# One-hots taken off VectorE, and 104 more gathered rows ordered ahead of the dense stage, in a decoder layer kernel

## The chip, the cores and the metric

The kernel runs on one core of a Trainium2 chip. The metric is the device time of one execution, in microseconds. The engines have short names here: PE is TensorE (the matmuls, with PEld its weight loads), DVE is VectorE, ACT is ScalarE, POOL is GpSimd, and SP is SyncE, which issues most plain DMAs. Each engine works through its own queue in order, and waits at an instruction until what that instruction needs has been done by the others.

## The reference

One decoder layer on 1024 tokens of width 1024: two kinds of attention in parallel, and then a retrieval layer with 16384 experts, each of which is one row of `peer_u` and one row of `peer_v`. Cut to what matters here:

```python
h = h + concat(mla(...), diff_attn(...)) @ w_out          # attention, 8 tiles of 128 tokens
x = rms_norm(h, ffn_norm)
# per token and head (8 heads): 16 experts out of 128 x 128, by a product of two lists of keys
best, flat = top_k(s1[..., :, None] + s2[..., None, :], 16)
experts = e1 * 128 + e2                                   # (token, 8 heads, 16)
g   = softmax(best)
act = gelu(einsum('cd,chkd->chk', x, u[experts]))         # 128 dot products per token
h   = h + einsum('chk,chkd->cd', g * act, v[experts])     # 128 weighted rows per token
```

So each token has 128 chosen experts, each with two keys `e1` and `e2` below 128 and a gate `g`.

## The kernel before

The 1024 tokens are 8 tiles of 128. The expert layer is done in two ways.

**Sparse tiles 0, 1, 6 and 7** (`sparse`, lines 938 to 983) gather the chosen rows. For each of the 128 choices, POOL issues an indirect DMA that brings one row of 1024 numbers to each of the 128 tokens (`gather`, line 957, 512 KB), and DVE makes the dot product with the token (`dot`, line 963); then the same over `peer_v`, where DVE adds the weighted row to a sum (`add`, line 975). One tile is a list of 259 entries: `begin`, 128 dots, `turn`, 128 adds, `end`. There are six row buffers, and two more in the dense stage, so POOL can run only that many rows ahead of DVE.

**Dense tiles 2 to 5** (`dense`, lines 985 to 1099) multiply all 512 tokens with all the experts on PE, 128 experts (one `e1`) at a time: 24 matmuls for the activations (line 1021) and 24 for the weighted sum (line 1055), each of 512 columns, 6144 in all. Around each `e1` DVE splits the loaded rows into high and low parts (lines 1017, 1043 and 1048) and multiplies by the gates (line 1039).

The dense stage needs the gates as a full table over (expert, token). `scatter` (lines 901 to 936) builds it ahead of that stage. For eight tokens at a time DVE compares `e2` with 0 to 127 (line 908, the tile `late_gq`, 128x1024). `place` then handles four tokens: for each it makes a one-hot of `e1` that is scaled by the gate (a 128x128 tile, `late_o`), and one matmul (line 928) of the two one-hots gives the token's gates; ACT copies the four results out (line 211, `late_st`), and from time to time SP stores them to the DRAM table `GD`. Of the four scaled one-hots one is made on POOL and two on DVE (both line 926), and one on ACT by a Square and a Relu (lines 923 and 924). There are 4 tiles x 32 places = 128 places, and eight `late_o` buffers, which is two places' worth.

**What sets the order.** The lists of work are woven together by `interleave`, in stages: `attend` and `mix` of the tile groups, projections, places, and a share of the sparse list. `some(share)` takes `int(share * 259)` more entries of the sparse list, by the table `SHARES`, as far as the tiles are ready. The program that the engines get is then ordered by a scheduler, which may put a row that is ready ahead of work that was written before it. The dense stage can start in earnest only when the last place has been stored. `choose` of tiles 6 and 7, the rest of the key search for those tiles, runs beside the last places and into the start of the dense stage; its small products on POOL have line 832.

Of the kernel before, what the change touches and what calls it, by code (L numbers as in the profile page):

```python
# [15 lines left out]
OP = mybir.AluOpType  # L16
# [37 lines left out]
PIN = 1  # L54
ROWS = 6
ROWS2 = 2
SHARES = [0.4,0.3,0.3,0.3,0.3,0.3,0.1,0.1]


def shape_constants():  # L60
# [34 lines left out]
def interleave(*streams):  # L95

    todo = []
    for st in streams:
        if st:
            c = [getattr(f, "cost", 1.0) for f in st]  # L100
            todo.append([0, 0.0, sum(c), list(st), c])
    total = sum(len(x[3]) for x in todo)
    for _ in range(total):
        x = min((x for x in todo if x[0] < len(x[3])), key=lambda x: (x[1] + x[4][x[0]]) / x[2])
        x[3][x[0]]()
        x[1] += x[4][x[0]]
        x[0] += 1
# [3 lines left out]
def layer(ctx, tc, a):  # L111
    nc = tc.nc
    ve, sc, pe, gp, sy = nc.vector, nc.scalar, nc.tensor, nc.gpsimd, nc.sync
# [59 lines left out]
    seg_start, seg_dstart, iota16, iota128 = c128[:, :16], c128[:, 16:32], c128[:, 32:48], c128[:, 48:]  # L173
# [36 lines left out]
    def evac(out, in_):  # L210
        sc.activation(out, in_, AF.Copy)  # L211
# [689 lines left out]
    def scatter(t):  # L901
        v = {}

        def one_hots(i0):

            full = [128, 8, 128]
            v["sq"] = GC(full)
            ve.tensor_tensor(v["sq"], iota128[:, None, :].to_broadcast(full),  # L908
                             ET[t][:, 1, i0:i0 + 8, None].to_broadcast(full), op=OP.is_equal)

        def place(i0):
            eT = ET[t]
            if i0 % STG == 0:
                v["st"] = ST()
            if i0 % 8 == 0:
                one_hots(i0)
            st, sq = v["st"], v["sq"][:, i0 % 8:i0 % 8 + 4]
            pg = MM().rearrange("p (i n) -> p i n", n=128)
            o1s = [O1() for _ in range(4)]
            for i in range(4):  # L920
                col = lambda n: eT[:, n, i0 + i:i0 + i + 1]
                if i == 1:
                    sc.activation(o1s[i], iota128, AF.Square, bias=col(3))
                    sc.activation(o1s[i], o1s[i], AF.Relu, bias=col(2), scale=col(4))
                else:
                    (ve if i else gp).tensor_scalar(o1s[i], iota128, col(0), col(2), op0=OP.is_equal, op1=OP.mult)  # L926
            for i in range(4):
                pe.matmul(pg[:, i], sq[:, i], o1s[i], start=True, stop=True)  # L928
            s0 = i0 % STG
            evac(st[:, :, s0:s0 + 4], pg.rearrange("p i e -> p e i"))  # L930
            if s0 == STG - 4:
                tg = (DENSE.index(t) * 128 + i0) // STG
                q, tg = divmod(tg, TD // STG // 4)
                sy.dma_start(GD[:, q, :, tg].rearrange("c p e i -> p c (e i)"),
                             st.rearrange("p (c e) i -> p c (e i)", e=GE))

        return [lambda i0=i0: place(i0) for i0 in range(0, 128, 4)]

    more_rows, n_row = [], [0]
# [160 lines left out]
    def first(kind, st):  # L1100
        off = HP.get(kind, 0)
        if not off:
            return st

        def run(f):
            with tc.high_priority(off):
                f()
        return [lambda f=f: run(f) for f in st]
# [23 lines left out]
    def some(share):  # L1132
        lo, done[0] = done[0], min(259 * sum(t in IDXED for t in SPARSE), done[0] + int(share * 259))
        return lookups[lo:done[0]]
# [13 lines left out]
    interleave(attend(GROUPS[0]) + mix(GROUPS[0], ch), P[1])  # L1148
    interleave(attend(GROUPS[1]), P[2] if last > 1 else [], some(SHARES[0]))
    d2 = []  # L1150
    for g in range(1, last + 1):
# [14 lines left out]
        def delayed(st, f):  # L1166
            return [lambda: None] * int(f * len(st) / (1 - f)) + st if f >= 0 else st + [lambda: None] * int(-f * len(st) / (1 + f))
        interleave(first("m%d" % g, delayed(mix(GROUPS[g]) + (picks(g) if g < last else []), MD)),
                   first("a%d" % g, delayed(attend(GROUPS[g + 1]), AD)) if g < last else [],
                   first("p%d" % g, delayed(P[g + 2], PD)) if g + 2 < len(P) else [], first("b%d" % g, wait + tt + made), some(SHARES[g]))  # L1170
    fin = [f for t in SPARSE if t not in IDXED for f in choose(t)]
# [51 lines left out]
```

## Time and profile before

| | us |
|---|---|
| median of 3 runs | 3104.34 |
| lowest and highest | 3099.56 and 3111.25 |
| the profiled execution | 3106.77 |
| its span, first to last instruction | 3104.9 |

Busy shares over the whole span: PE 91%, PE weight loads 68%, DVE 81%, ACT 32%, POOL 57%. These are averages over stages with different limits. A windows table gives, for stretches of the span, the busy time of every engine with the number of its instructions in brackets, and then the granted TensorE clock (1.00 is 2.4 GHz), the share of time that the DMA engines were busy, and their GB/s. A group of instructions has a line of the kernel, an engine, an operation, `out<-in` names, shapes and a count; then busy time and the mean length of one in ns; and behind the bar the time that the engine stood idle just ahead of them, with what ended it.

### The profile page before, as it was taken

The numbers are of one execution on the slowest core, as the hardware profiler recorded it, in microseconds if no ns is written. First come the engines' busy times: TensorE is split into PE (matmuls) and PEld (weight loads), VectorE is DVE, ScalarE is ACT, GpSimd is POOL, SyncE is SP. The second block draws the span as 40 slices with busy tenths as digits, with TensorE's granted clock in tenths as the row PEclk, the third lists the DMA queues.
The fourth block names the chain that finished last, engine by engine and source line by source line (L and its number), as shares of the span: only waits on it lengthen the run. The fifth ranks groups of instructions, "written<-read, shape, count | busy, mean of one in ns | idle before, by whom it ended". The sixth has DMA issues, their size and how long they took to land.

```text
span 3104.9 us, 38301 instructions
## 1 busy us (share of the span) xinstructions
PE 2834.8 (91%) x12574; PEld 2125.7 (68%) x12574; DVE 2509.4 (81%) x5183; ACT 1002.0 (32%) x2030; POOL 1766.8 (57%) x1405
## 2 busy tenths in 40 slices
PE   7897889998897796889887999999999999999997
PEld 2555455565655673577676888788888877888885
DVE  1238775788999889976998997988888879888898
ACT  1413333322332342245573223222222222232221
POOL 2116673556557755741585764765555547666565
PEclk9698878998998897789998999999999999999998
DMA  7369897989989988954658998999999989999998
GB/s 214 108 236 312 300 328 254 347 304 315 324 282 319 316 303 269 333 182 149 214 170 288 350 361 311 342 374 346 338 351 342 351 278 386 350 351 342 339 345 312
DMA packets 371951, 934.35 MB, mean 301 GB/s; under 512 B 53365, under 2 KB 134393, under 8 KB 371753
## 3 DMA queue, kind: packets, MB, share of 16 engines
q0 software_dynamic: 147456, 536.94, 48.1%
q1 hardware_dynamic: 224296, 394.98, 37.0%
q8 instruction: 99, 1.62, 0.2%
q14 instruction: 100, 0.81, 0.1%
HBM read 871.80 MB, written 59.99 MB: 300 GB/s over the span
## 4 chain that ended last, share of the span: by engine, by line
PE 57%; DVE 16%; DMA 5%; issue 4%; POOL 3%; ACT 1%; DVEq 0%; POOLq 0%; ACTq 0%; SPq 0%
PE pa L1021 21%; PE acc L1055 16%; PE pa L1055 5%; PE mm L748 3%; DVE row L963 3%; PE sc L564 2%; PE mm L359 2%; DVE acc L975 2%; POOL row L957 2%; DVE late_o L926 2%; DMA row<-in_peer_u,idx 2%; DVE late_gq L908 1%; PE mm L594 1%; PE mm L928 1%; DMA skt<-in_sub_keys_t 1%
## 5 line engine op out<-in xcount | busy, mean ns | idle before, releaser
L957 POOL DMA_INDIRECT row<-in_peer_v,idx x512 | 680.3, 1329 | 479.5 <-DVE acc L975 312.5
L957 POOL DMA_INDIRECT row<-in_peer_u,idx x512 | 689.3, 1346 | 421.0 <-DVE row L963 224.7
L975 DVE SCALAR_TENSOR_TENSOR acc<-row,w,acc 128x1024 f32<-128x1024 f32 x512 | 668.6, 1306 | 10.4 <-DMA row<-in_peer_v,idx 5.9
L963 DVE SCALAR_TENSOR_TENSOR row<-row,xn 128x1024 f32<-128x1024 f32 x512 | 624.3, 1241 | 33.3 <-DMA row<-in_peer_u,idx 31.7
L1021 PE MATMUL pa<-xTh,us 128*128 128x512 f32 x2048 | 501.2, 393 | 17.0 <-DVE us L1017 15.1
L1021 PEld LDWEIGHTS pa<-xTh,us 128*128 128x128 f32 x2048 | 387.8, 190 | 100.0 <-DVE us L1017 16.2
L1055 PE MATMUL acc<-vh,al 128*128 128x512 f32 x768 | 301.7, 393 | 10.2 <-DVE al L1043 10.2
L1037 ACT ACTIVATE ga<-pa 128x512 f32<-128x512 f32 x128 | 76.6, 598 | 710.9 <-PE pa L1021 707.4
L1055 PE MATMUL acc<-vl,ah 128*128 128x512 f32 x768 | 300.6, 391 | 0.0
L1055 PE MATMUL acc<-vh,ah 128*128 128x512 f32 x768 | 270.1, 391 | 5.0 <-ACT ah L1042 5.0
L748 PE MATMUL mm<-xyT,slab 128*128 128x256 f32 (+1 forms) x1280 | 255.2, 353 | 5.5 <-DMA slab<-in_peer_w_query 4.4
L1021 PE MATMUL pa<-xTl,us 128*128 128x512 f32 x1024 | 254.6, 390 | 0.0
L359 PE MATMUL mm<-slab,nT 128*128 128x512 f32 x512 | 239.1, 613 | 1.0 <-ACT pc L211 0.9
L564 PE MATMUL sc<-kh,qh 96*128 96x512 f32 (+9 forms) x416 | 191.6, 574 | 49.1 <-ACT p L576 36.8
L748 PEld LDWEIGHTS mm<-xyT,slab 128*128 128x128 f32 x1280 | 212.4, 200 | 34.7 <-DMA slab<-in_peer_w_query 6.3
L926 POOL TENSOR_SCALAR late_o<-c,eT 128x128 f32<-128x128 f32 x128 | 148.1, 1160 | 137.2 <-PE mm L928 135.8
L1021 PEld LDWEIGHTS pa<-xTl,us 128*128 128x128 f32 x1024 | 193.5, 189 | 40.6
L1017 DVE TENSOR_TENSOR us<-raw,us 128x1024 fp32r<-128x1024 f32 x128 | 157.5, 1230 | 66.5 <-PE pa L1021 39.9
L1047 ACT ACTIVATE vh<-rv 128x1024 fp32r<-128x1024 f32 x128 | 132.8, 1053 | 191.1 <-PE pa L1055 143.5
L205 POOL TENSOR_TENSOR y<-v,neghalf 128x8 f32<-128x8 f32 (+6 forms) x68 | 92.8, 1365 | 173.1 <-DVE v L204 169.2
L1055 PEld LDWEIGHTS acc<-vh,al 128*128 128x128 f32 x768 | 145.2, 189 | 43.9 <-DVE al L1043 13.7
L928 PE MATMUL mm<-late_o,late_gq 128*128 128x128 f32 x1024 | 150.2, 291 | 23.4 <-POOL late_o L926 8.0
(249 smaller groups left out, 4651.1 us busy)
## 6 DMA issues: line engine op xcount, KB each, us to landing
raw<-in_peer_u_t SPq DMA_DIRECT2D x128, 512.0 KB, 6.7
rv<-in_peer_v SPq DMA_DIRECT2D x128, 512.0 KB, 6.8
slab<-in_peer_w_query SPq DMA_DIRECT2D x80, 512.0 KB, 7.5
slab<-in_w_in SPq DMA_DIRECT2D x64, 512.0 KB, 6.9
GD<-late_st SPq DMA_DIRECT2D x16, 2048.0 KB, 9.5
gc<-GD SPq DMA_DIRECT2D x16, 2048.0 KB, 14.7
slab<-in_w_out SPq DMA_DIRECT2D x40, 512.0 KB, 6.6
row<-in_peer_u,idx POOLq DMA_INDIRECT x512, 7.4
```

The lines of the kernel that those rows point to most:

```text
L359: pe.matmul(p, nT[t][:, k], w(k), start=(k == 0), stop=(k == 7))
L564: pe.matmul(at(lo, hi), qt, kt[:, lo:hi], start=True, stop=not ex)
L748: pe.matmul(p, w["q"](k)[:, j * 128:j * 128 + 128], st["xT"][:, k, :NG], start=(k == 0), stop=(k == 7))
L926: (ve if i else gp).tensor_scalar(o1s[i], iota128, col(0), col(2), op0=OP.is_equal, op1=OP.mult)
L928: pe.matmul(pg[:, i], sq[:, i], o1s[i], start=True, stop=True)
L957: gp.indirect_dma_start(out=r, out_offset=None, in_=a[name], in_offset=bass.IndirectOffsetOnAxis(ap=IDX[t][:, j:j + 1], axis=0))
L963: ve.scalar_tensor_tensor(r, r, 1.0, v["x"], op0=OP.mult, op1=OP.mult, accum_out=v["act"][:, j:j + 1])
L975: ve.scalar_tensor_tensor(v["y"], r, wj, v["y"], op0=OP.mult, op1=OP.add)
L1017: ve.tensor_tensor(ul, ur, uh.bitcast(F32), op=OP.subtract)
L1021: pe.matmul(pa, l[:, k], r[:, k], start=(i == 0 and k == 0), stop=(i == 2 and k == 7))
L1047: sc.activation(vh, vr, AF.Copy)
L1055: pe.matmul(out, l[:, ts], r[:, hf:hf + 512], start=(first and n == 0), stop=(last and n == 2))
```

## The change

Two things. `SHARES` gives other shares of the sparse list to the stages ahead of the dense one: 103 + 90 + 90 + 103 + 129 = 515 entries where it was 103 + 4 x 77 = 411. Entry 515 is the 126th add of tile 1, so 510 of the 512 rows of tiles 0 and 1 are written ahead, against 406 before. And in `place` the two scaled one-hots that DVE made go elsewhere: tokens 0 and 2 to POOL, tokens 1 and 3 to ACT.

```diff
-SHARES = [0.4,0.3,0.3,0.3,0.3,0.3,0.1,0.1]
+SHARES = [0.4,0.35,0.35,0.4,0.5]
@@ place
-                if i == 1:
+                if i % 2:
                     sc.activation(o1s[i], iota128, AF.Square, bias=col(3))
                     sc.activation(o1s[i], o1s[i], AF.Relu, bias=col(2), scale=col(4))
                 else:
-                    (ve if i else gp).tensor_scalar(o1s[i], iota128, col(0), col(2), op0=OP.is_equal, op1=OP.mult)
+                    gp.tensor_scalar(o1s[i], iota128, col(0), col(2), op0=OP.is_equal, op1=OP.mult)
```

In POOL's queue, around the 75th of the 128 places (line 832 is the key search, line 926 a one-hot, line 957 a gathered row of tile 1), before:

```order
L926 TENSOR_SCALAR late_o_12303<-c_94,eT 128x128
L926 TENSOR_SCALAR late_o_12323<-c_94,eT 128x128
L832 TENSOR_TENSOR oh<-oh,d_13665 128x512
L926 TENSOR_SCALAR late_o_12338<-c_94,eT 128x128
L926 TENSOR_SCALAR late_o_12370<-c_94,eT 128x128
L832 TENSOR_TENSOR oh<-oh,d_13665 128x512
```

The same place in POOL's queue of the changed kernel:

```order
L957 DMA row<-in_peer_v,idx_6579 128x1024
L926 TENSOR_SCALAR late_o_12583<-c_94,eT 128x128
L957 DMA row<-in_peer_v,idx_6579 128x1024
L926 TENSOR_SCALAR late_o_12585<-c_94,eT 128x128
L957 DMA row<-in_peer_v,idx_6579 128x1024
L832 TENSOR_TENSOR oh<-oh,i1f 128x512
L926 TENSOR_SCALAR late_o_12614<-c_94,eT 128x128
L957 DMA row<-in_peer_v,idx_6579 128x1024
L926 TENSOR_SCALAR late_o_12616<-c_94,eT 128x128
```

Two one-hots for each place stand where one stood, with rows of tile 1 between them. From the first row of tile 1's adds to the last one-hot, POOL's queue held 28 rows, 110 one-hots, 28 products of line 832 and 4 of line 205; now it holds 132 rows, 220 one-hots and the same 28 and 4.

DVE's queue at the last places, before:

```order
L908 TENSOR_TENSOR late_gq<-c_94,eT 128x1024
L926 TENSOR_SCALAR late_o_13381<-c_94,eT 128x128
L926 TENSOR_SCALAR late_o_13382<-c_94,eT 128x128
L908 TENSOR_TENSOR late_gq<-c_94,eT 128x1024
L926 TENSOR_SCALAR late_o_13398<-c_94,eT 128x128
L926 TENSOR_SCALAR late_o_13399<-c_94,eT 128x128
```

The same place now:

```order
L908 TENSOR_TENSOR late_gq<-c_94,eT 128x1024 x4
L762 MAX s_12383<-qc 128x8 x4
L764 MAX_INDEX i_12384<-s_12383,qc 128x8 x4
L766 MATCH_REPLACE qc<-s_12383,qc 128x128 x4
L908 TENSOR_TENSOR late_gq<-c_94,eT 128x1024
L768 MAX s_12383<-qc 128x8 x4
L770 MAX_INDEX i_12384<-s_12383,qc 128x8 x4
L908 TENSOR_TENSOR late_gq<-c_94,eT 128x1024 x9
```

DVE is left with the comparison for each eight tokens; no one-hot of line 926 is in its queue any more.

DVE's queue at the end of the program, before:

```order
L1069 TENSOR_TENSOR yacc<-yacc,pa 128x512 x2
L975 SCALAR_TENSOR_TENSOR acc_22411<-row_24443,w,acc_22411 128x1024
L975 SCALAR_TENSOR_TENSOR acc_22411<-row_24452,w,acc_22411 128x1024
L975 SCALAR_TENSOR_TENSOR acc_22411<-row,w,acc_22411 128x1024 x6
L975 SCALAR_TENSOR_TENSOR acc_22411<-row_24515,w,acc_22411 128x1024
L975 SCALAR_TENSOR_TENSOR acc_22411<-row_24522,w,acc_22411 128x1024
L1076 TENSOR_TENSOR rv<-rv,acc 128x1024
```

Now:

```order
L1039 TENSOR_TENSOR ga<-ga,gc 128x512
L1043 TENSOR_TENSOR al<-ga,ah 128x512
L1076 TENSOR_TENSOR rv<-rv,acc 128x1024 x2
L1069 TENSOR_TENSOR yacc<-yacc,pa 128x512 x2
L1076 TENSOR_TENSOR rv<-rv,acc 128x1024
```

The ten adds behind the last dense sum are gone from the end: the last row of tile 7 now stands some 18 of the 128 `e1` steps ahead of it.

## Rows read from the trace of the kernel before

**Rows 1.** Windows by stage: us, busy time of each engine (instructions), clock, DMA
```profile
1018.00:1258.00 240.00, 189.99 (x941) 142.24 (x940) 214.95 (x709) 80.16 (x192) 153.40 (x116) 0.85 0.88 297
1258.00:1641.00 383.00, 327.54 (x1992) 275.22 (x1991) 316.19 (x1011) 207.63 (x504) 212.31 (x170) 0.91 0.62 203
1641.00:1710.00 69.00, 49.91 (x196) 39.07 (x195) 60.15 (x166) 21.04 (x27) 34.92 (x22) 0.85 0.84 304
1710.00:3084.00 1374.00, 1360.75 (x5962) 1121.71 (x5960) 1204.45 (x1431) 384.89 (x493) 840.44 (x597) 0.99 0.93 344
```

**Rows 2.** Chain that ended last, in order of time: start, length, what (steady dense stage)
```profile
2049.43 5.44 PE pa L1021 x24
...
2103.38 4.08 PE acc L1055 x18
```

**Rows 3.** Groups of POOL from 1258 to 1641: busy, mean ns, idle before
```profile
L926 POOL TENSOR_SCALAR late_o<-c,eT 128x128 f32<-128x128 f32 x110 | 126.1, 1150 | 126.2 <-PE mm L928 125.2
L957 POOL DMA_INDIRECT row<-in_peer_v,idx x28 | 38.2, 1363 | 17.6 <-DVE acc L975 4.5 <-issue 3.6 <-DVE t L206 2.6
L832 POOL TENSOR_TENSOR oh<-oh,i1f 128x512 f32<-128x512 f32 x16 | 23.9, 1496 | 7.4 <-DVE oh L830 6.6 <-DVE t L206 0.6
L832 POOL TENSOR_TENSOR oh<-oh,d 128x512 f32<-128x512 f32 x12 | 20.7, 1725 | 11.8 <-DVE oh L830 11.8
L205 POOL TENSOR_TENSOR y<-v,neghalf 128x1 f32<-128x1 f32 (+1 forms) x4 | 3.8, 954 | 7.6 <-DVE v L204 7.6
```

**Rows 4.** Lines 926 and 957: count, shortest/median/longest ns, first and last start
```profile
L926 POOL TENSOR_SCALAR late_o<-c,eT x128: 780/871/2697, 1017.8 to 1639.8; 128x128 f32<-128x128 f32 x128
L957 POOL DMA_INDIRECT row<-in_peer_v,idx x512: 932/1144/4012, 590.6 to 3090.2; - x171
```

**Rows 5.** Windows of line 926 alone: us, DVE busy, POOL busy, clock, DMA
```profile
1018.00:1100.00 82.00, 5.39 (x16) 12.48 (x9) 0.85 0.88 302
...
1340.00:1486.00 146.00, 22.48 (x73) 37.64 (x38) 0.93 0.46 146
...
1591.00:1641.00 50.00, 19.83 (x62) 39.81 (x30) 0.97 0.56 174
```

**Rows 6.** Timeline of POOL in the last places: start, length, what
```profile
1624.50 0.87 POOL L926 TENSOR_SCALAR late_o<-c,eT 128x128 f32<-128x128 f32 x1 [0.73 <-PE mm L928]
1625.62 4.43 POOL L926 TENSOR_SCALAR late_o<-c,eT 128x128 f32<-128x128 f32 x3 [0.25 <-PE mm L928]
```

**Rows 7.** Timeline of DVE there
```profile
1624.88 0.60 DVE L926 TENSOR_SCALAR late_o<-c,eT 128x128 f32<-128x128 f32 x2 [1.03 <-PE mm L928]
1625.40 1.22 DVE L908 TENSOR_TENSOR late_gq<-c,eT 128x1024 f32<-128x1024 f32 x1
1626.54 1.11 DVE L926 TENSOR_SCALAR late_o<-c,eT 128x128 f32<-128x128 f32 x4
1627.56 1.22 DVE L908 TENSOR_TENSOR late_gq<-c,eT 128x1024 f32<-128x1024 f32 x1
```

**Rows 8.** Groups of DVE from 1258 to 1641
```profile
L926 DVE TENSOR_SCALAR late_o<-c,eT 128x128 f32<-128x128 f32 x220 | 77.5, 391 | 39.9 <-PE mm L928 39.7
L908 DVE TENSOR_TENSOR late_gq<-c,eT 128x1024 f32<-128x1024 f32 x54 | 65.6, 1215 | 0.0
L830 DVE TENSOR_TENSOR oh<-pf,c 128x512 f32<-128x512 f32 x28 | 19.1, 683 | 0.2
```

**Rows 9.** Groups of ACT from 1258 to 1641
```profile
L924 ACT ACTIVATE late_o<-late_o,eT 128x128 f32<-128x128 f32 x110 | 53.5, 487 | 0.5
L923 ACT ACTIVATE late_o<-c,eT 128x128 f32<-128x128 f32 x110 | 43.8, 398 | 17.2 <-PE mm L928 16.3
```

**Rows 10.** Costliest groups of the page: the adds of the gathered rows
```profile
L975 DVE SCALAR_TENSOR_TENSOR acc<-row,w,acc 128x1024 f32<-128x1024 f32 x512 | 668.6, 1306 | 10.4 <-DMA row<-in_peer_v,idx 5.9
```

**Rows 11.** Timeline of DVE and SP at the end
```profile
3085.25 1.27 DVE L1069 TENSOR_TENSOR yacc<-yacc,pa 128x512 f32<-128x512 f32 x2
3086.44 13.31 DVE L975 SCALAR_TENSOR_TENSOR acc<-row,w,acc 128x1024 f32<-128x1024 f32 x10
...
3099.68 1.21 DVE L1076 TENSOR_TENSOR rv<-rv,acc 128x1024 f32<-128x1024 f32 x1
...
3100.91 0.33 SPq L1077 DMA_DIRECT2D out<-rv  x1
```

## The prediction

> **What bounds the kernel now.** I read the windows by stage first [rows 1]. From 1710 to 3084 us PE is busy 1360.8 of 1374 us: the dense stage is PE's. The chain of waits says the same: in the steady part it is one run of matmuls after another, 24 in 5.44 us and 18 in 4.08 us, that is 0.2267 us each [rows 2]; 6144 of them are 1393 us. DVE is busy 1204 of 1374 us there, under PE, so a gathered row taken out of this stage is worth nothing by itself. It can only shorten what PE waits (13 us from 1710 on, 19 us in the run-up from 1641) and what follows PE's last sum. Ahead of 1641 no engine is full: PE 327, DVE 316, ACT 208 and POOL 212 of 383 us. That stretch runs from the first row of tile 1's adds (1258) to the last one-hot (1641), and the dense stage stands behind its end. POOL has 171 us to spare in it, and 125 us of that it waits for PE to give back a `late_o` buffer [rows 3]: POOL is ahead there and others set the pace.
>
> **POOL's queue, the main term.** In that stretch POOL's queue held 28 rows, 110 one-hots, 28 products of line 832 and 4 of line 205. The order of the changed kernel gives it 132 rows and 220 one-hots (places 19 to 128, two each), and the same 28 and 4. Priced at what this very stretch shows [rows 3]: 220 x 1.150 = 253 us, 132 x 1.363 = 180, the products 23.9 + 20.7 = 45, line 205 4, and the gap of 0.13 us per row that the group calls issue (3.6 us for 28) 17: 499 us in a stretch of 383. So POOL turns from an engine with slack into the one that sets the pace, unless its instructions get much shorter.
>
> What does a one-hot cost in the new surroundings? Its median is 871 ns but its longest 2697 [rows 4]. The windows of this line show when: 37.64 / 38 = 0.99 us from 1340 to 1486, where no rows are gathered; 12.48 / 9 = 1.39 between rows, from 1018 to 1100; 39.81 / 30 = 1.33 in the last places, where the comparisons follow fast [rows 5]. The timelines show the mechanism: a POOL one-hot takes 0.87 us while DVE does one-hots, and the next three take 4.43 us while DVE does two comparisons of 1.22 us: 4.43 - 3 x 0.87 = 1.8 of those 2.4 us were added to POOL [rows 6, 7]. DVE's one-hots themselves do not do that. So a DVE instruction with two operands in memory holds up POOL's, and in the new order a comparison or an add of a row runs beside POOL nearly everywhere. I take 1.30, nearer to 1.33 and 1.39: 220 x 1.30 = 286, and the sum is 286 + 180 + 17 + 45 + 4 = 532 us. To it come POOL's waits for DVE, which were 18.4 + 7.6 + some 13 us in this stretch [rows 3]; DVE has fewer small things to do, so I keep half, 20. The waits for buffers go, since the slowest engine does not wait for the others: 552 us in place of 383, **+169 us**. Ends: 499 (+116) with the old mean and no waits; 631 (+248), below, if DVE blocks in full.
>
> The Trainium skill, "SBUF — State Buffer", Who interferes with whom, states such a rule: GpSimd reads through a port that it shares with VectorE, a VectorE instruction with two inputs in SBUF contends with a GpSimd instruction that reads SBUF, and the later one waits for the whole of the other. The trace agrees in direction, with 1.8 of 2.4 us [rows 6, 7]. It speaks against this change, which puts the one-hots on POOL and the two-input adds of the rows beside them; taken to the letter it gives the third rival below.
>
> **The other engines in that stretch.** DVE loses 220 one-hots, 77.5 us [rows 8], and gains 104 adds of 1.306 us, 136 us [rows 10]: 316 becomes 374, under 552. ACT gains 110 pairs of Square and Relu, 0.49 + 0.40 us: 53.5 + 43.8 = 97 us [rows 9], so 208 becomes 305; also covered. Only at the end, with no rows left, does ACT come near POOL, and both are then slower than DVE was. The rows bring 104 x 0.52 MB = 55 MB to a stretch where the DMA engines are busy 0.62 of the time [rows 1], and the stretch gets longer: nothing. If POOL's cover were gone, DVE's 374 us would be next, about what the stretch takes now.
>
> **The stretch before, 1018 to 1258.** 18 more one-hots on POOL (at 1.3: 23 us) and 36 fewer on DVE (36 x 0.391 = 14 us) [rows 8]. POOL is busy 153 of 240 us, DVE 215 [rows 1]. DVE is nearer the bound, but POOL pays: I take 0, with -14 to +23.
>
> **The dense stage.** 104 adds of tile 1 leave it for the stretch before, 136 us of DVE work off an engine that has 170 us to spare: PE's 1393 us stay. In the order the rows are done as fast as DVE may, and end some 18 `e1` steps early. PE's run-up and stalls (19 + 13 us [rows 1]) I leave as they are: DVE has less queued, but tile 6's first 17 dots (17 x 1.2 = 21 us) now stand between two splits of line 1017 four steps into the stage, where PE needs one every 10.9 us (48 x 0.2267). Range -15 to +15. What does go is the tail: behind PE's last sum DVE does ten adds in 13.31 us before the last output can leave [rows 11], and in the changed queue none stands there. The add of line 1076 and its store follow at once: **-13 us**.
>
> **Sum.** The profiled execution took 3106.8 us with what lies around its span; 3106.8 + 169 - 13 = 3263. It is 2.4 us above the median of the three runs, so **3260 us** against 3104.3, 5.0% slower. Its own range: low with 499 us in the main stretch, -14 before it and -15 in the dense stage (3106.8 + 116 - 14 - 13 - 15 - 2.4 = 3178), high with 1.39 per one-hot and all 39 us of waits (+20 + 19), +23 and +15, not all at once: 3310.
>
> **Rivals.** *POOL keeps up.* If each record falls to its median (0.871 and 1.144 us [rows 4]), POOL needs 192 + 151 + 17 + 45 + 4 = 409 us, +26: 3106.8 + 26 - 13 - 2.4 = 3117, 0.4% slower, no change that can be told. For it: from 1340 to 1486 one-hots run at 0.99. Against: no rows ran there, and rows are what the change brings. *The other side: DVE is the true bound, and relieving it pays.* With POOL at its shortest (0.780 and 0.932: 172 + 123 + 17 + 45 + 4 = 361 us) DVE's 374 us decide, and if nothing else waits the stretch ends 9 us early; with -14 before it, the tail -13 and half of PE's 32 us of dense stalls, 3106.8 - 9 - 14 - 13 - 16 - 2.4 = 3052. It decides from where POOL's queue falls under some 370 us, an average one-hot under 0.82; only 1.15 was seen here. *POOL is blocked in full.* If every two-input instruction of DVE in the stretch stops POOL for its whole length, 126 adds x 1.306 + 54 comparisons x 1.215 + 28 x 0.683 = 250 us [rows 8, 10] come on top of the shortest 361, and with 20 us of waits the stretch takes 631: 3106.8 + 248 - 13 - 2.4 = 3339. For it: 1.8 of 2.4 us in the timeline. Against: the rows of this stretch take 1.363 with DVE 83% busy, not 0.93 + 1.3, so descriptors are not stopped in full. *The change does not do what it says:* two of the 512 rows stay behind, which is 5 us at most and no case of its own.
>
> **How the numbers follow.** Forecast 0.68, POOL blocked in full 0.17, POOL keeps up 0.08, DVE relieved 0.07. The time is the forecast's, 3260. Its 3178 to 3310 holds most of 0.68; the upper rival is taken in up to 3340, and some of the way towards POOL keeping up: 3160 to 3340. Within 0.5% (16 us, about what a measurement of this kernel can tell from no change): 0.08. Faster 0.07, slower 0.85.
>
> **What would show it.** POOL over 90% busy from the first row of tile 1's adds to the last one-hot, that stretch near 550 us, one-hots of 1.25 us or more, PE and DVE waiting for line 926 in place of POOL waiting for line 928; the dense stage as long as before, with its end right behind PE. Wrong would be one-hots near 0.87 us among the rows, or a stretch that stays under 430 us; or PE gaining in the dense stage by more than its 32 us of waits, which it can't by these rows.

## The result, and the profile after

The changed kernel takes **3257.74 us** (median of four runs, 3255.53 to 3259.35) against 3107.3 us for the kernel before beside it: ratio 1.0487, 95% interval 1.0463 to 1.051. The prediction said 3260 in a range of 3160 to 3340. The profiled execution's span is 3253.4 us, before 3104.9.

First the windows by stage of the changed kernel, cut at the first row of tile 1's adds and at the last one-hot on POOL, with the same 69 and 1374 us behind them as in [rows 1]; PE's last sum ends at 3242.8. Columns: the stretch, its us, busy us of PE, PEld, DVE, ACT and POOL with instruction counts, the granted clock, the DMA share and GB/s.

```profile
1018.00:1263.50 245.50, 199.33 (x946) 148.62 (x947) 205.02 (x673) 88.02 (x220) 166.03 (x133) 0.82 0.86 286
1263.50:1798.00 534.50, 386.55 (x1988) 318.95 (x1986) 387.38 (x913) 285.32 (x724) 469.42 (x384) 0.78 0.77 248
1798.00:1867.00 69.00, 53.97 (x197) 42.34 (x198) 58.18 (x156) 20.21 (x27) 33.37 (x21) 0.85 0.78 279
1867.00:3241.00 1374.00, 1358.59 (x5949) 1119.71 (x5949) 1096.29 (x1327) 385.73 (x494) 707.21 (x498) 1.00 0.84 308
3241.00:3254.00 13.00, 1.83 (x9) 1.17 (x7) 3.56 (x4) 0.00 (x0) 0.00 (x0) 0.75 0.58 202
```

The main stretch (383 us in [rows 1]) is the one that grew, to 534. In the dense stage DVE lost 108 us of work (1204 to 1096 in 1374 us) and PE did not move (1360.8 to 1358.6): the rows taken out of there were hidden, and stayed worth nothing.

POOL's two big groups in the main stretch, as in [rows 3] (busy us, mean ns, idle before and its releasers), and then the waits of that stretch (us, times, longest):

```profile
L926 POOL TENSOR_SCALAR late_o<-c,eT 128x128 f32<-128x128 f32 x220 | 265.7, 1214 | 9.3 <-PE mm L928 6.9
L957 POOL DMA_INDIRECT row<-in_peer_v,idx x126 | 155.7, 1236 | 46.5 <-issue 16.9 <-DVE acc L975 8.3 <-DVE c L638 2.9
```
```profile
PEld mm L928 <- POOL late_o L926: 115.0, 84, 7.9
PE mm L928 <- POOL late_o L926: 92.9, 68, 7.7
DVE late_gq L908 <- PE mm L928: 81.2, 27, 8.5
...
DVE acc L975 <- DMA row<-in_peer_v,idx: 30.3, 16, 6.5
```

PE's wait for POOL in the kernel before, in the same stretch:

```profile
PE mm L928 <- POOL late_o L926: 8.0, 14, 1.9
```

Before, POOL waited 125 us for PE to free a `late_o` buffer [rows 3]. Now that wait is 6.9 us, and it is PE that waits for POOL's one-hots, 92.9 us in 68 waits where it waited 8.0; DVE's comparisons in turn wait for PE. So POOL has gone from waiting to being waited for. But it is not full on average: 469 of 534 us, 88%. Cutting the stretch in two, at the 64th of the 128 groups of four tokens ("places": one call of `place` each), shows why (columns as above, the changed kernel):

```profile
1263.50:1602.60 339.10, 253.18 (x1264) 204.20 (x1262) 278.52 (x717) 156.53 (x393) 281.19 (x218) 0.80 0.87 289
1602.60:1797.80 195.20, 133.35 (x723) 114.70 (x723) 108.67 (x196) 128.59 (x332) 188.23 (x167) 0.75 0.59 178
```

The same two parts in the kernel before:

```profile
1258.10:1528.80 270.70, 231.57 (x1271) 187.21 (x1269) 212.65 (x723) 121.90 (x296) 118.69 (x98) 0.89 0.63 209
1528.80:1640.70 111.90, 95.56 (x717) 87.65 (x718) 103.15 (x287) 85.44 (x208) 93.62 (x73) 0.97 0.60 189
```

In **part 1**, where 105 of the 132 rows stand, POOL is busy 281 and DVE 279 of 339 us: 83% and 82%, neither full. Each waits for the other at times (a row must be gathered before DVE adds it, and a buffer added before POOL gathers the next):

```profile
DVE acc L975 <- DMA row<-in_peer_v,idx: 19.5, 10, 5.1
...
POOL row L957 <- DVE acc L975: 8.3, 6, 2.2
```

These two waits are 28 of the 118.5 us that DVE and POOL together are idle there; the rest is many small waits. In **part 2** the rows run out and POOL is full: 188 of 195 us, 96%. Part 1 grew by 68 us and part 2 by 83. The windows of line 926 alone give the price of a one-hot in each:

```profile
1263.50:1602.60 339.10, 127.39 (x93) 0.80 0.87 289
1602.60:1797.80 195.20, 138.30 (x128) 0.75 0.59 178
```

1.37 us in part 1 and 1.08 in part 2. A one-hot on which a two-operand instruction of DVE lies from its start, or from its first 0.2 us, is dear (the experiments show this below); by the trace's records there are 59 such of 93 one-hots in part 1, and 55 of 127 in part 2, where DVE's comparisons wait for PE and PE for POOL.

Last, the end (start, length, what, idle before):

```profile
3242.42 1.28 DVE L1069 TENSOR_TENSOR yacc<-yacc,pa 128x512 f32<-128x512 f32 x2 [0.36 <-PE pa L1055]
...
3248.39 1.22 DVE L1076 TENSOR_TENSOR rv<-rv,acc 128x1024 f32<-128x1024 f32 x1 [4.69 <-DMA rv<-hd]
3249.64 0.33 SPq L1077 DMA_DIRECT2D out<-rv  x1
```

The ten adds of [rows 11] are gone from behind PE's last sum. What is late next is the reload of `rv`, which the adds used to cover: DVE waits 4.69 us for it.

### The profile page after: what moved, and what is told of

It is laid out like the page before. It is cut to its first block, busy times and chain, and to the rows that moved or that the text cites. A ratio compares the mean times of both kernels' runs of the same rounds, so it can differ in the third digit from the quotient of the medians.

```text
span 3253.4 us, 38439 instructions
## 1 busy us (share of the span) xinstructions
PE 2904.6 (89%) x12574; PEld 2176.0 (67%) x12574; DVE 2449.7 (75%) x4927; ACT 1089.4 (33%) x2286; POOL 1897.3 (58%) x1533
## 4 chain that ended last, share of the span: by engine, by line
PE 53%; POOL 10%; DVE 9%; issue 7%; DMA 6%; ACT 2%; SPq 0%; POOLq 0%; DVEq 0%; ACTq 0%
PE pa L1021 19%; PE acc L1055 15%; POOL late_o L926 5%; PE pa L1055 5%; POOL row L957 3%; DMA row<-in_peer_u,idx 3%; PE sc L564 3%; DVE row L963 2%; PE mm L359 2%; PE mm L594 2%; PE mm L748 2%; DVE acc L975 2%; PE mm L716 1%; PE mm L928 1%; DMA row<-in_peer_v,idx 1%
## 5 line engine op out<-in xcount | busy, mean ns | idle before, releaser
L957 POOL DMA_INDIRECT row<-in_peer_v,idx x512 | 657.9, 1285 | 434.8 <-DVE acc L975 259.2
L926 POOL TENSOR_SCALAR late_o<-c,eT 128x128 f32<-128x128 f32 x256 | 315.3, 1237 | 23.2 <-PE mm L928 20.2
L928 PE MATMUL mm<-late_o,late_gq 128*128 128x128 f32 x1024 | 197.0, 339 | 109.4 <-POOL late_o L926 94.0
L748 PE MATMUL mm<-xyT,slab 128*128 128x256 f32 (+1 forms) x1280 | 266.4, 364 | 13.3 <-DMA slab<-in_peer_w_query 7.0
L928 PEld LDWEIGHTS mm<-late_o,late_gq 128*128 128x128 f32 x1024 | 165.4, 237 | 135.3 <-POOL late_o L926 118.8
L748 PEld LDWEIGHTS mm<-xyT,slab 128*128 128x128 f32 x1280 | 222.4, 210 | 43.8 <-DMA slab<-in_peer_w_query 8.9
L1021 PEld LDWEIGHTS pa<-xTl,us 128*128 128x128 f32 x1024 | 195.2, 191 | 41.1
```

Of the source, the lines that this page charges most:

```text
L748: pe.matmul(p, w["q"](k)[:, j * 128:j * 128 + 128], st["xT"][:, k, :NG], start=(k == 0), stop=(k == 7))
L926: gp.tensor_scalar(o1s[i], iota128, col(0), col(2), op0=OP.is_equal, op1=OP.mult)
L957: gp.indirect_dma_start(out=r, out_offset=None, in_=a[name], in_offset=bass.IndirectOffsetOnAxis(ap=IDX[t][:, j:j + 1], axis=0))
L1021: pe.matmul(pa, l[:, k], r[:, k], start=(i == 0 and k == 0), stop=(i == 2 and k == 7))
```

## The experiments

The theory on trial: POOL's queue sets the length of the main stretch, and its one-hots are dear because DVE's instructions with two operands in memory hold POOL up. The rivals: the rows alone, or DVE, make the length; or it makes no difference what runs beside a one-hot. Rows alone, one-hots alone, the same with the comparison split, and ACT two, DVE one stood on one chip beside the kernel before at 3111.15 us; POOL three, ACT three, the changed kernel with the comparison split and the sixteen rows on a second, beside 3110.14; the last two of the table on a third, beside a single execution of 3125.62. The stages are compared from one trace of each kernel. Six times are of one execution each: both split comparisons, POOL three, ACT three, and the two with DVE one. The kernel before spread from 3096 to 3126 us over its executions, so a difference of 10 or 20 us between two of these six, in the time or in a stretch, is near what chance can do.

| kernel | time | main stretch | part 1 | part 2 | POOL one-hot, mean | one-hots of four on POOL / ACT / DVE | rows |
|---|---|---|---|---|---|---|---|
| before | 3107.3 | 382.5 | 270.7 | 111.9 | 1.150 | 1 / 1 / 2 | 28 |
| after | 3257.74 | 534.3 | 339.1 | 195.2 | 1.214 | 2 / 2 / 0 | 126 |
| rows alone | 3187.5 | 465.1 | 305.0 | 160.1 | 1.420 | 1 / 1 / 2 | 126 |
| one-hots alone | 3154.33 | 420.2 | 283.6 | 136.6 | 1.038 | 2 / 2 / 0 | 28 |
| the same, comparison split | 3117.53 | 403.8 | 279.0 | 124.8 | 0.877 | 2 / 2 / 0 | 28 |
| ACT two, DVE one | 3125.2 | 403.2 | 280.6 | 122.6 | 1.074 | 1 / 2 / 1 | 28 |
| after, POOL three | 3332.05 | 610.3 | 374.4 | 235.8 | 1.084 | 3 / 1 / 0 | 126 |
| after, ACT three | 3224.71 | 512.8 | 329.7 | 183.1 | 1.329 | 1 / 3 / 0 | 126 |
| after, comparison split | 3230.4 | 520.4 | 335.4 | 185.0 | 1.016 | 2 / 2 / 0 | 126 |
| after, DVE one in part 2 | 3222.33 | 495.1 | 334.3 | 160.9 | 1.369 | 2 / 2 / 0, then 1 / 2 / 1 | 126 |
| after, DVE one in part 1 | 3198.58 | 509.9 | 323.5 | 186.4 | 1.124 | 1 / 2 / 1, then 2 / 2 / 0 | 126 |

Stretches in us, each cut at its own events; "rows" are the adds' rows issued inside it.

**The rows alone.** The kernel before with the new shares:

```
-SHARES = [0.4,0.3,0.3,0.3,0.3,0.3,0.1,0.1]
+SHARES = [0.4,0.35,0.35,0.4,0.5]
```

> The new shares alone; one-hots as before (one POOL, one ACT, two DVE). Theory (POOL's queue, held up by DVE's two-input instructions, sets the stretch from tile 1's first add to the last one-hot, 534 us in the changed kernel): POOL now has 126 rows and 110 one-hots there, about 126 x 1.36 + 16 + 110 x 1.25 + 49 = 375 us, so POOL is no longer the limit; DVE has 316 + 104 x 1.306 = 452 us, so DVE is, and with some 25 us of waits the stretch takes 475: 3107 + 92 - 10 = about 3190. Rival (the rows alone cost what the change costs, the one-hots nothing): 3250. Rival (the rows are hidden in idle time, the one-hots do all the harm): 3095 to 3110.

Measured: 3187.5 us, ratio 1.027 (1.023 to 1.0311), near the 3190 of the theory. The stretch grew by 82.6 us for 98 more rows, 0.84 us a row, and its two parts show the fullest engine (columns as above):

```profile
1256.70:1561.70 305.00, 250.04 (x1267) 201.88 (x1266) 287.73 (x776) 123.58 (x297) 213.15 (x161) 0.83 0.91 300
1561.70:1721.80 160.10, 112.69 (x719) 100.50 (x719) 151.44 (x330) 90.44 (x208) 152.09 (x106) 0.86 0.80 236
```

DVE 94% in part 1 and 95% in part 2. With DVE still doing half of the one-hots, the rows make DVE the fullest engine, and about half of the whole loss is there without any change of the one-hots. What PE is seen to wait for is POOL's one-hot all the same:

```profile
PE mm L928 <- POOL late_o L926: 50.1, 33, 3.6
...
PE mm L928 <- DVE late_o L926: 3.0, 6, 1.4
```

That DVE's load is what delays POOL there is read from the 94%, not shown by a wait.

**The one-hots alone.** The kernel before with the new assignment:

```
-                if i == 1:
+                if i % 2:
-                    (ve if i else gp).tensor_scalar(...)
+                    gp.tensor_scalar(...)
```

> The one-hots moved alone (two POOL, two ACT, none DVE); shares as before. Theory: POOL has 28 rows and 220 one-hots in the stretch, 28 x 1.36 + 4 + 220 x 1.2 + 49 = 355 us, plus 40 us of waits for DVE: 395 in place of 383, the tail stays: about 3120, and one-hots stay over 1.1 us since DVE's comparisons still run beside them. Rival (the one-hots alone do the harm): 3220 or more. Rival (DVE was the limit and is relieved by 85 us): 3060.

Measured: 3154.33 us, ratio 1.0156 (1.0125 to 1.0188); the expectation was too low, the stretch took 420 where about 395 was expected, though the one-hots came out cheaper, at 1.038 and not over 1.1. The two parts of the stretch:

```profile
1266.40:1550.00 283.60, 233.79 (x1275) 188.61 (x1273) 191.01 (x652) 155.02 (x398) 168.04 (x150) 0.89 0.62 206
1550.00:1686.60 136.60, 111.78 (x714) 96.79 (x713) 64.26 (x157) 122.21 (x328) 135.10 (x131) 0.91 0.46 145
```

Part 2 shows why: POOL is busy 135.1 of 136.6 us and ACT 122.2. The two halves of the change, +37.7 and +82.6, make 120 of the 152 us; the other 32 come only when both are there.

**What holds POOL up.** The same kernel with the comparison of eight tokens, one instruction with two operands in memory, written as eight with one such operand and a scalar:

```
-            ve.tensor_tensor(v["sq"], iota128..., ET[t][:, 1, i0:i0 + 8, None]..., op=OP.is_equal)
+            for j in range(8):
+                ve.tensor_scalar(v["sq"][:, j], iota128, ET[t][:, 1, i0 + j:i0 + j + 1], None, op0=OP.is_equal)
```

> The one-hots moved alone, and the comparison of eight tokens on DVE (one instruction with two operands in memory, 1.22 us) made as eight instructions with one operand in memory and a column, as DVE's own one-hots were. Theory (an instruction of DVE with two operands in memory holds up POOL): the mean one-hot on POOL falls from about 1.2 us in the run with the one-hots moved alone to 0.95 or less, while DVE's time for the comparisons doubles to 54 x 2.6 = 140 us. Rival (POOL's one-hots are slow among DVE's work whatever its form, or the records are loose): the mean stays at 1.15 or more.

The groups of both lines in the main stretch, of the kernel with the one-hots alone, then of this one:

```profile
L926 POOL TENSOR_SCALAR late_o<-c,eT 128x128 f32<-128x128 f32 x220 | 226.0, 1038 | 75.5 <-PE mm L928 75.2
L908 DVE TENSOR_TENSOR late_gq<-c,eT 128x1024 f32<-128x1024 f32 x54 | 68.4, 1267 | 111.7 <-PE mm L928 111.5
```
```profile
L926 POOL TENSOR_SCALAR late_o<-c,eT 128x128 f32<-128x128 f32 x220 | 190.3, 877 | 92.2 <-PE mm L928 91.9
L909 DVE TENSOR_SCALAR late_gq<-c,eT 128x128 f32<-128x128 f32 x432 | 100.4, 304 | 75.5 <-PE mm L928 75.4
```

DVE does 32 us more for the same result (68.4 to 100.4), less than the doubling that was expected, and yet the kernel is 37 us faster, 3117.53 against 3154.33; 16 of the 37 lie in the main stretch and 15 ahead of it. POOL's one-hots, whose code is the same, fell from 1.038 to 0.877 us.

The traces settle what the edit alone leaves open, whether it is the operands or the length of DVE's instruction. Each POOL one-hot of the main stretch was sorted by what ran on DVE during it; "two operands" are DVE's instructions TENSOR_TENSOR and SCALAR_TENSOR_TENSOR.

| kernel | no two-operand instruction beside it | one that starts over 0.2 us into the one-hot | one under way at its start, or starting within 0.2 us |
|---|---|---|---|
| one-hots alone | 107, mean 0.788 | 40, mean 0.790 | 73, mean 1.541 |
| the same, comparison split | 185, mean 0.852 | 16, mean 0.855 | 19, mean 1.135 |
| after | 80, mean 0.788 | 26, mean 0.790 | 114, mean 1.609 |

So it is the two-operand form on DVE that makes POOL slow, and only where it is there first. DVE's load does so hardly (0.852 against 0.788, where DVE's one-operand work lies beside 154 of the 185), nor does the length of its instruction: six one-hots of the split kernel lay beside a one-operand instruction of over 0.9 us, and took 0.816 on average. In the kernel before, where DVE's own one-hots stand in between, the middle group is less clean: 14, mean 1.111.

The same edit in the changed kernel:

> The changed kernel with the comparison of eight tokens split into eight instructions with one operand in memory. Theory: the comparison no longer holds POOL up, only the adds of the rows do: the mean one-hot in the stretch falls from 1.21 to about 1.0 us, POOL's queue to some 450 us; DVE has 387 - 70 + 143 = 460. The stretch falls to 480 to 500, though DVE has 73 us more to do: about 3210. Rival (POOL is held up by the adds alone): one-hots stay at 1.2 and the time at 3255 or above.

```profile
L926 POOL TENSOR_SCALAR late_o<-c,eT 128x128 f32<-128x128 f32 x220 | 222.1, 1016 | 21.3 <-PE mm L928 19.1
```
```profile
1255.40:1590.80 335.40, 261.94 (x1280) 208.48 (x1278) 298.53 (x874) 155.33 (x391) 259.60 (x219) 0.81 0.90 294
1590.80:1775.80 185.00, 128.97 (x721) 111.11 (x721) 125.28 (x412) 126.54 (x330) 171.42 (x166) 0.76 0.62 187
```

3230.4 us, 27 less than the changed kernel, and the one-hots at 1.016 in place of 1.214, as the mechanism has it. The gain stays behind the expectation: POOL's one-hots are 265.7 - 222.1 = 44 us shorter, but the stretch only 14 (8 more lie ahead of it). In part 1 DVE now has 299 of 335 us, and its adds, still with two operands, remain; that this is why is not shown.

**How the stretch hangs on POOL.** The changed kernel with three of four one-hots on POOL and one on ACT (`i == 1`, the rest on `gp`):

> The changed kernel with three one-hots on POOL and one on ACT. Theory (POOL's queue sets the main stretch one for one): 110 more one-hots in it at the 1.21 us that the changed kernel shows are 133 us, and 18 more in the stretch before add 10 to 20: about 3400. ACT loses 97 us, which would show if ACT set the pace. Rival (the chain over ACT's Square and Relu, or the rows and DVE, set it): 3257 or less.

and with one on POOL and three on ACT (`if i:`):

> The changed kernel with one one-hot on POOL and three on ACT. Theory: POOL has 372 us in the stretch, DVE 387 and ACT 285 + 97 = 382, all near each other; with waits the stretch falls from 534 to 430 to 460: 3150 to 3185. Rival (the rows beside the places cost the time, whoever makes the one-hots): 3230 or more.

In both the effect was smaller than expected. Three on POOL: 3332.05 us, the stretch 76 us longer for 110 more one-hots, 0.69 us each, not 1.2 or more. One on POOL: 3224.71, the stretch only 21.5 us shorter for 110 fewer. The parts, of POOL three and then of ACT three:

```profile
1266.40:1640.80 374.40, 277.57 (x1248) 217.09 (x1247) 290.13 (x731) 127.82 (x298) 324.51 (x268) 0.76 0.83 266
1640.80:1876.60 235.80, 160.35 (x728) 131.56 (x728) 105.89 (x214) 96.74 (x208) 230.40 (x227) 0.66 0.44 137
```
```profile
1249.60:1579.30 329.70, 264.49 (x1309) 208.19 (x1308) 298.37 (x721) 183.27 (x488) 257.43 (x187) 0.84 0.96 318
1579.30:1762.40 183.10, 135.75 (x712) 117.28 (x712) 86.56 (x175) 160.69 (x448) 108.18 (x89) 0.75 0.51 159
```

With three on POOL it is full in part 2 (98%) and 87% in part 1. Its busy time grew by 85.5 us (469.4 to 554.9), not by 133, as the mean one-hot fell to 1.084: the stretch grew by 0.89 us for each us more of POOL's time, so what was too high here is mostly the price of a one-hot. With three on ACT, POOL's busy time fell by 104 us and the stretch by 21.5. POOL has 75 us to spare in part 2 there and ACT is at 88%; in part 1 DVE is at 90%. PE's waits in part 2 still name POOL more than ACT, so that ACT has become what sets the pace is not shown:

```profile
PE mm L928 <- POOL late_o L926: 31.7, 17, 8.2
...
PE mm L928 <- ACT late_o L924: 6.2, 26, 0.7
```

Beside the rows alone, which has the same 110 one-hots on POOL and 86 us more of one-hots on DVE, ACT three is slower by 48 us of stretch. So moving DVE's one-hots on to ACT did not pay either.

This broke the simple form of the theory, POOL alone and one for one in both directions, and the next two runs tried what I put in its place, one edit in two places: of each four one-hots one goes back to DVE (1 POOL, 2 ACT, 1 DVE), in the second pair of dense tiles only, or in the first pair only.

```
-                    gp.tensor_scalar(...)
+                    (ve if i and DENSE.index(t) > 1 else gp).tensor_scalar(...)
```

> The changed kernel, with one scaled one-hot of each four given back to DVE, in the second pair of dense tiles only (the last 64 of the 128 places). If POOL sets the pace of the whole main stretch, one for one, 64 one-hots of 1.21 us less on it take 77 us off the stretch: 457 us, and a time near 3176. If the stretch is two parts, a first one where DVE is full and a second one where POOL and ACT are, the second one, 195 us from place 64 on, comes down until ACT's two one-hots of each four hold it: the 82 us to place 80, which still have rows, lose 16 x 1.21 = 19, and the 115 us behind come to the 92 that ACT took for the same places where DVE had one one-hot and the old shares stood. Stretch near 492, time near 3212, the first 64 places as long as before (339 us).

The first pair had `DENSE.index(t) < 2` in the same place:

> The same edit in the other half: one scaled one-hot of each four given back to DVE in the first pair of dense tiles only (places 1 to 64; some 46 of these one-hots lie in the main stretch). If POOL sets the pace of the whole stretch, one for one, 46 x 1.21 = 56 us go: stretch 478, time near 3198. If DVE is what is full in the part with the rows, the 46 one-hots cost DVE 46 x 0.39 = 18 us there while POOL gains room that nobody uses: the first 64 places stay within -10 and +18 us of their 339, the stretch is 524 to 552, and the time 3243 to 3272.

The parts, of the edit in part 2 and then of the edit in part 1:

```profile
1264.50:1598.80 334.30, 255.03 (x1273) 206.13 (x1271) 276.27 (x701) 156.24 (x392) 281.02 (x217) 0.82 0.88 291
1598.80:1759.70 160.90, 118.80 (x714) 106.64 (x715) 122.83 (x255) 123.33 (x326) 138.89 (x104) 0.82 0.75 220
```
```profile
1235.10:1558.60 323.50, 254.19 (x1296) 200.35 (x1294) 295.51 (x749) 155.57 (x392) 229.53 (x178) 0.85 0.94 312
1558.60:1745.00 186.40, 126.48 (x723) 110.26 (x723) 103.25 (x216) 128.13 (x334) 178.81 (x162) 0.79 0.57 176
```

In part 2 the two-part reading held: stretch 495 (492 expected, 457 by one for one), part 1 as long as before the edit. Part 2 gained 34 us for 64 one-hots and then no engine was full, POOL 86% and ACT 77%. In part 1 neither theory held: part 1 is 15.6 us shorter, outside the -10 to +18 of "DVE is full" and far from the 56 of "POOL sets the pace". The whole stretch lost 24 us for 46 one-hots, 0.53 us each. That the time of 3198.58 agrees with the 3198 of "POOL sets the pace" is chance: of the 59 us that it lies under the changed kernel, 8 lie ahead of the first one-hot, where the edit changes nothing, and 20 between that and the first row of tile 1's adds (248 to 228 us), which neither theory had counted. I read this as POOL and DVE sharing the pace in part 1, where POOL went from 83% to 71% and DVE from 82% to 91%; with one execution and 15.6 us it is not shown.

**Two tries at a faster kernel.** The kernel before with two one-hots on ACT, one on POOL, one on DVE (`i == 1` becomes `i % 2` alone):

> Shares as before; one-hots: one on POOL, one on DVE, two on ACT. Theory: POOL's queue is as before, DVE has 38 us less and ACT 97 us more (305 of 383): no engine is made the limit, and DVE's waits shrink a little: 3080 to 3107. Rival (ACT's place in the chain matters and its Square and Relu make the places late): 3120 or more.

3125.2 us, ratio 1.0054 (1.0029 to 1.0079): no gain, as the rival had it. The stretch grew by 21 us, although each of the four one-hots stands on the engine that seemed to have room; what in it grew was not found. And the kernel before with sixteen-odd rows more ahead of the dense stage, to cut only the tail:

```
-SHARES = [0.4,0.3,0.3,0.3,0.3,0.3,0.1,0.1]
+SHARES = [0.45,0.3,0.3,0.3,0.3]
```

> The kernel before with 0.45 for the first share: 13 more entries ahead, which the order puts as 16 more rows in the main stretch, and 4 adds in place of 25 after the last but one split of DVE. Theory: the tail behind PE falls by 8 to 10 us, and the rows cost the stretch some 0.84 us each (82.6 us for 98 rows in the run with the new shares alone), 13 us: 3107 to 3115, no gain. Rival (the first rows find DVE idle and are free): 3095 to 3100.

3125.29 us, ratio 1.0041 (1.0015 to 1.0067): no gain, and 10 us beyond the 3107 to 3115. The tail fell from 20.9 to 10.3 us, as in the changed kernel, but the main stretch took 399.9 us, 17 more, and from there to PE's last sum 1454.9, 11.5 more. None of the ten kernels beat the one before.

## Why the prediction was right, and where its reading was not

The time was right within 2.3 us, which is in part luck: the executions of the kernel before alone lie up to 12 us apart, and the terms miss by more and cancel:

| term | predicted | measured |
|---|---|---|
| main stretch | +169 (383 to 552) | +151.8 (382.5 to 534.3) |
| - one-hots on POOL, 220 | 286 at 1.30 | 265.7 at 1.214 |
| - rows, 132 | 180 at 1.363 | 155.7 + 6.7 = 162.4 |
| - line 832 | 45 | 22.4 + 15.7 = 38.1 |
| - POOL's gaps and waits | 17 + 20 | 534.3 - 469.4 = 64.9 |
| from 1018 to that stretch | 0 (-14 to +23) | +5.4 |
| dense stage | 0 (-15 to +15) | +1.6 |
| behind PE's last sum | -13 | -10.3 |

The sum is +148.5 us of span, where +156 was forecast; the row "from 1018" and the dense stage add 7 us that the forecast took at 0.

**The main step held, with two errors that nearly cancel.** POOL's instructions were priced 45 us too high and its idle time 28 us too low. One-hots: 1.39 was taken from between rows and 1.33 from the last places [rows 5]. The first was right, 1.37 in part 1. The second fell to 1.08. In the old last places (1591 to 1641) 14 of 30 one-hots had a two-operand instruction beside them, at 1.89 us on average; in part 2 now 55 of 127 have one from their start, at 1.48. So the share is about the same and each is held up less. I read this as an effect of order: DVE's comparisons now wait for what POOL feeds (81 us of waits of line 908 for PE), and some start when a one-hot is already under way and do not hold it up (12 in part 2, 0.79 us); it was not tested. The waits: POOL's waits for DVE were halved because "DVE has fewer small things to do". The waits for buffers did go (125 to 6.9 us), and the gaps of issue came as priced (18.5), but POOL stood idle for 46 us more, and 58 of its 65 us of idle time lie in part 1, where no engine is full.

**What the prediction misread** is why 552. It had one engine set the pace for the whole stretch and covered DVE's 374 us under it. DVE did 387 and ACT 285 (305 forecast), so the sums were sound, but a mean over the stretch hides that 102 of DVE's 126 adds lie in part 1, and that POOL is full only in part 2. Two of its signs came out short: "POOL over 90% busy" was 88%, made of 83 and 96, and "one-hots of 1.25 us or more" was 1.214. The runs put numbers on that, in us of the whole stretch for each one-hot: 110 more on POOL cost 0.69, 64 taken off in part 2 gave 0.61, 46 in part 1 0.53, and 110 moved to ACT 0.20. For each us of POOL's busy time it is 0.89 when time is added, and 0.79, 0.40 and 0.21 when it is taken away: POOL's queue is nearly the length when more is put on it, and less and less so when it is relieved. Read as "POOL's queue is the length", the prediction's own working would have given 1.2 to 1.3 for each one-hot, and the expectations for POOL three and ACT three, built on it, were too large. What share of a one-hot's time counts in part 1, and why the two halves of the change cost 32 us more together than apart, is not settled.

**The blocking was right in kind and nearly in size; that it is partial was a misreading.** It is now shown by the split comparison, not only by a timeline [rows 6, 7]: 1.038 to 0.877, and 1.214 to 1.016. The third rival, blocked in full, would have laid 250 us of two-input work on 344 us of POOL instructions at their shortest (361 less the 17 of gaps). POOL was busy 469.4 us, so half of it counted, 125 us, by this estimate. The prediction took the blocking itself as partial, 1.8 of 2.4 us. In fact the two comparisons lay on the three one-hots for 2.2 us only, from 1625.62 on, and at the shortest one-hot of 0.78 [rows 4] 2.1 of that was added: where DVE is first, POOL is held up almost in full. What made the sum smaller is that many two-operand instructions run while POOL waits, or start behind a running one-hot, which costs nothing (0.790 us). The Trainium skill, "SBUF — State Buffer", Who interferes with whom, says of a VectorE instruction with two inputs in SBUF and a GpSimd instruction that reads SBUF that whichever issues first has the shared port for its whole length and the other waits. For a one-hot that comes second the trace of the changed kernel agrees (1.609 us against 0.788); for DVE it does not, since the 34 comparisons that started over 0.1 us into a one-hot took 1.234 us on average there, against 1.215 before [rows 8].

**The other engines.** The dense stage stayed as it was with 108 us less on DVE, as forecast: that stage is PE's. Before the main stretch, where 18 more one-hots stand on POOL, the time grew by 5 us, inside the bound; the run that gave DVE one of four back in the first pair was 20 us shorter there.

**The tail** was 3 us short. Its step said that the add of line 1076 and its store follow at once when the ten adds are gone. They wait 4.69 us for the reload of `rv`, which those adds had covered.

**The rivals.** None came. "POOL keeps up" needed one-hots near 0.87 us; the mean comes to that only with little two-operand work beside them, as the split comparison showed. "DVE relieved" failed twice: neither kernel that took one-hots off DVE under the old shares, one-hots alone and ACT two with DVE one, was faster for it.

## What to carry to other kernels

A stage in which no engine is full on average can still be full by parts: cut it where the mix of work changes and read the busy shares there, before moving work to the engine "with room". Moving element work from VectorE to GpSimd costs more than GpSimd's price alone (1.609 us against 0.788 here) if VectorE's two-operand instructions are under way when it starts; writing those with a scalar operand can pay even when they get slower. And work taken off an engine that hides under another buys nothing, while the engine that it is moved to can become the one that the others wait for.

## What the runs showed of the hardware that I had not expected

- The same one-operand POOL instruction (128x128, f32) took 1.420 us on average in the kernel with the rows alone, 1.038 with the one-hots alone, and 0.877 where the comparisons beside it had one operand in memory: a factor of 1.6 for code that did not change. Sorted one by one in the changed kernel, it took 0.788 without a two-operand DVE instruction beside it, 0.790 with one that started over 0.2 us later, and 1.609 with one that was there first.
- POOL's issue of a gathered row (line 957) is held up as well: over the whole kernel before it took 0.952 us on average in the 88 cases without a two-operand DVE instruction beside it, and 1.374 in the other 936.
- Eight DVE instructions of 128x128 with one operand in memory took 1.9 us of DVE for eight tokens (100.4 / 54) against 1.27 for the one of 128x1024 with two, and were the better choice while POOL was full.
- PE's busy time in the main stretch rose from 327.5 to 386.6 us for the same matmuls (x1992 and x1988), with the granted clock at 0.91 before and 0.78 after, 0.97 and 0.75 in part 2: PE, made to wait for POOL, was granted the lower of its two levels (1.2 and 2.4 GHz) more of the time. Each place passes through PE, so this may be part of what POOL's slowness cost; whether and how much was not tried.
